# Last query and value stores on GpSimd's queue, the keys' rotation ahead of two reversed differences, and row differences one group sooner

## The chip, the core and the metric

The kernel runs on one core of one Trainium2 chip. The metric is device time in microseconds (us) of one execution. A core has a matrix engine (TensorE, "PE"), a vector engine ("DVE"), a scalar engine ("ACT"), GpSimd ("POOL") and SyncE ("SP"). Each of them works through its own list of instructions in order, and they wait for each other through semaphores. Transfers between the chip's memory (DRAM) and the on-chip memory (SBUF) are issued here by SP, ACT and POOL. Matrix products land in PSUM, in tiles (banks) of 128 partitions by 512 words.

## What is computed

The reference is one layer of a diffusion backbone, for 256 prompt tokens and 2048 latent tokens of width 1024. One projection gives queries, keys, values and Fourier channels. Four heads run differential attention; four groups of 128 channels go through a two-dimensional Fourier transform; both are joined, projected, and followed by a squared-ReLU MLP. Only these parts bear on the change:

```python
def project(h, w_in, q_g, k_g):
    p = h @ w_in
    q, k, v, f = jnp.split(p, [QK_WIDTH, 2 * QK_WIDTH, 2 * QK_WIDTH + ATTN_WIDTH], axis=-1)
    q = rms_norm(q.reshape(b, n, N_HEADS, 2, HEAD_DIM), q_g)
    k = rms_norm(k.reshape(b, n, N_HEADS, 2, HEAD_DIM), k_g)
...
def fourier_mix(f, w_four):
    spec = jnp.fft.fft2(f.astype(jnp.float32), axes=(1, 3), norm='ortho').real.astype(f.dtype)
    return jnp.einsum('bngc,gce->bnge', spec, w_four).reshape(b, n, FOUR_WIDTH)
```

Latent queries and keys are also rotated by their grid position ("axial rotary").

## The kernel before

The work is done in stages that follow each other on PE: setup and projection (to about 485 us), the Fourier transform (to about 559 us), attention, output projection and MLP. Each operand of a large product is split into a high and a low part (`hi` by a cast on ACT, `lo` by a subtraction on DVE), and `mm3` (lines 86 to 89) runs three products.

**Projection.** Tokens come in 18 tiles of 128. For each tile, `proj` (line 238) makes four 512-column groups: 0 queries, 1 keys, 2 values, 3 Fourier channels. `qk_norm` (266) and `qk_post` (272) normalise and rotate queries and keys on DVE: a small table product (292), a product (293), two half products (301) and an addition (303). `head_T` transposes them; `k_store` (317) and `q_store` (328) write the parts to DRAM, four and eight transfers of 128 KB, in pieces of 512 bytes. `v_post` (360) copies the values out of PSUM, splits them and issues three stores (357, 349).

**The last tile** (lines 560 to 649) has its order written out by hand. `manual_schedule()` fixes, for each engine, that the instructions of the region go in the order in which they are written. The region that follows (789 onward) has an order of its own; how the two are merged on an engine is left to the scheduler. In this stretch POOL loads the cosine and sine matrices of the 2048-point transform (`c_load`, `dft`, line 583), 512 KB each. SP loads the Fourier rows (`d_load`, 599) and stores keys and queries of the tile before the last (`k_store`, `q_store`, lines 619 and 620).

**Even and odd parts.** `e2048(t)` (624) takes a row tile and its mirror image `rv` and makes, on DVE, their difference (628) and sum (629), the sum in place of the mirror. ACT casts the difference (634), and DVE subtracts (635): the operands `E_h`, `E_l`. For t = 0, POOL copies one row into the sum (631). The tiles are taken in the order 3, 2, 0, 1 (`EROWS`).

**Fourier stage.** PE first multiplies the four even parts (line 827), for four channel groups, into four banks (`pabE`), and makes the group matrices (807, 808) in a fifth (`pabw`). The pool `ab` has five banks. The sums are split into `O_h`, `O_l` (831, by the helper at 578 and 579), first t = 0, the one with POOL's row. Then `e_evac` and `group_parts` empty banks, and the loop over groups (845) runs the odd products into a bank `pabo` (846). Meanwhile POOL loads ten smaller matrices (838), SP the prompt's rows (841) and eight tiles of row sums (`s_load`, 732). These eight share buffers with the cosine matrices, so each pair waits until PE has read the matrix before it.

**Preparation** for the shorter transforms is a list, `PREP` (774), of which `prep(n)` takes the next n entries: the prompt's two splits, four row differences (`diff`, 741), reversals by matrix product on PE (`reverse`, 755 and 756), sums (744), and even and odd parts made from the reversals (764, 765). The loop over groups calls `prep(2)` for g = 1 and 3; later loops call `prep(3)` for each prompt group and `prep(1)` for each later group (871). The stage ends where attention's first scores begin (line 969).

Of the kernel before, what the change touches and what calls it, by code (L numbers as in the profile page):

```python
# [19 lines left out]
P = 128  # L20
# [6 lines left out]
H = 4  # L27
# [10 lines left out]
def f32(ap):  # L38
    return ap.bitcast(F32)


def body(tc, a, out):
    nc = tc.nc
    ctx = ExitStack()
    with ctx:
# [6 lines left out]
        def scratch(name, shape):  # L52
            return dram.tile(shape, F32, tag=name, name=name)
# [3 lines left out]
        vs = scratch("vs", [NS, 512])  # L57
        NK = (PAST + NS, NP)
        kd = [scratch(f"kd{s}", [H, 2, P, NK[s]]) for s in range(2)]
        vd = [scratch(f"vd{s}", [H, P, NK[s] // P, 2, P]) for s in range(2)]  # L60
        qd = [scratch(f"qd{s}", [H, (NS, NP)[s] // 256, P, 2, 2, 256]) for s in range(2)]
# [24 lines left out]
        def mm3(ps, lh, ll, rh, rl, first, last):  # L86
            nc.tensor.matmul(ps, lh, rh, start=first, stop=False)  # L87
            nc.tensor.matmul(ps, lh, rl, start=False, stop=False)  # L88
            nc.tensor.matmul(ps, ll, rh, start=False, stop=last)  # L89
# [119 lines left out]
        with ExitStack() as c1:  # L209
# [6 lines left out]
            def t2(nm):  # L216
                return p1.tile([P, 512], F32, tag="t2", name=nm, bufs=6)

            def t2r(nm):
                return po.tile([P, 512], F32R, tag="t2r", name=nm, bufs=6)  # L220
# [17 lines left out]
            def proj(i, g):  # L238
                ps = pp.tile([P, 512], F32, tag="pj", name=f"pj{i}_{g}", bufs=4)
                hh, hl = HH[i]  # L240
                for k in range(KD):
                    mm3(ps, hh[:, k, :], hl[:, k, :], wh[g][k], wl[g][k], k == 0, k == KD - 1)
                PJ[i, g] = ps
# [81 lines left out]
                n = i if s else i - 2  # L325
                k_store(s, n if s else 4 + n, head_T(QK[i][1], f"kT{i}"))

            def q_store(i, hl):
                s = 1 if i < 2 else 0
                n = i if s else i - 2  # L330
                for m in range(2):
                    for x in range(2):
                        for d in range(2):
                            nc.sync.dma_start(qd[s][:, n // 2, d * 64:d * 64 + 64, x, m, n % 2 * P:n % 2 * P + P]
                                              .rearrange("h p k -> p h k"), hl[x][m * 64:m * 64 + 64])

            def q_T(i):
# [3 lines left out]
                k_T(i)  # L341
                q_T(i)

            def v_split(s, kt, src, nm):
                hi, lo = t2r(f"{nm}h"), t2r(f"{nm}l")
                nc.scalar.copy(hi, src)
                nc.vector.tensor_sub(lo, src, f32(hi))
                for x, t in enumerate((hi, lo)):
                    nc.sync.dma_start(vd[s][:, :, kt, x, :].rearrange("h p e -> p h e"), f32(t).rearrange("p (h e) -> p h e", h=H))

            def v_out(i):
                s = 1 if i < 2 else 0
                n = i if s else i - 2
                ps = PJ.pop((i, 2))
                o = t2(f"vo{i}")
                nc.scalar.copy(o, ps)
                nc.sync.dma_start(out[3][n * P:n * P + P] if s else vs[n * P:n * P + P], o)
                return o

            def v_post(i):  # L360
                s = 1 if i < 2 else 0
                n = i if s else i - 2
                o = v_out(i)
                v_split(s, n if s else 4 + n, o, f"v{i}")

            FH = {}

# [159 lines left out]
            wm, LAST = None, N1 - 1  # L527
# [32 lines left out]
            with tc.manual_schedule():  # L560
                rope_load(LAST)
                f_load(LAST)
                f_rev(LAST - 1)
                proj(LAST, 3)
                f_post(LAST)
                parts = [head_T(QK[LAST - 1][m], f"qkT{LAST - 1}_{m}") for m in (1, 0)]
                proj(LAST, 0)
                squares(LAST, 0, True)
                proj(LAST, 1)
                right.close()  # L570
                fa = right.enter_context(tc.tile_pool(name="f_a", bufs=2, side="right", reuse_waits="tile"))

                def ft32(pool, tag, nm, bufs):
                    return pool.tile([P, 512], F32, tag=tag, name=nm, bufs=bufs)

                def split(src, nm):
                    hi, lo = (ft32(fa, "src", f"{nm}{x}", 16).bitcast(F32R) for x in "hl")
                    nc.scalar.copy(hi, src)
                    V.tensor_sub(lo, src, f32(hi))
                    return hi, lo  # L580

                def dft(m, nm, t):
                    nc.gpsimd.dma_start(m, a[nm][t * P:t * P + P])
                    return m[:, 0, :], m[:, 1, :]


                ROWS, EROWS = (0, 1, 2, 3), (3, 2, 0, 1)
                src0 = [ft32(fa, "src", f"E{t}_{x}", 16) for t in EROWS for x in "hl"]
                etmp = [ft32(fa, "e", f"etmp{n}", 2) for n in range(2)]
                qko = [ft32(fa, "qo", f"qo{LAST}_{m}", 2) for m in range(2)]  # L590
                som = {t: fa.tile([P, 2, 512], F32R, tag="so", name=f"s2048{t}", bufs=4) for t in ROWS}
                DR = {t: (ft32(fa, "ds", f"ds{t}", 4), ft32(fa, "rv", f"rv{t}", 4)) for t in EROWS}
                com = {t: fa.tile([P, 2, 512], F32R, tag="co", name=f"c2048{t}", bufs=4) for t in EROWS}
                co, so = [None] * 4, [None] * 4
                c128, s128 = (fa.tile([P, P], F32, tag=x, name=x, bufs=1) for x in ("c128", "s128"))
                wf = fa.tile([P, 4, P], F32, tag="wf", name="wf", bufs=1)

                def d_load(t, x):
                    nc.sync.dma_start(DR[t][x], (fdif, frev)[x][t * P:t * P + P])

                def c_load(t):
                    co[t] = dft(com[t], "c2048", t)


                f_rev(LAST)
                for t in (3, 2):
                    d_load(t, 0)
                    d_load(t, 1)
                    c_load(t)
                nc.gpsimd.dma_start(c128, a["c128"])  # L610
                nc.gpsimd.dma_start(s128, a["s128"])
                nc.gpsimd.dma_start(wf, a["w_four"][0].rearrange("g p c -> p g c"))
                c_load(0)
                mid = p1.tile([P, 512], F32, tag="ff", name="mid", bufs=4)
                nc.sync.dma_start(mid[0:1, :], fdif[512:513])
                for x in range(2):
                    for t in (0, 1):
                        d_load(t, x)
                k_store(0, LAST + 1, parts[0])
                q_store(LAST - 1, parts[1])  # L620

                E, O = {}, {}

                def e2048(t):

                    d, r = DR[t]
                    e = t2(f"e2048_{t}")
                    V.tensor_sub(e, d, r)
                    V.tensor_add(r, d, r)
                    if t == 0:  # L630
                        nc.gpsimd.tensor_copy(r[0:1, :], mid[0:1, :])
                    n = 2 * EROWS.index(t)
                    hi, lo = (x.bitcast(F32R) for x in src0[n:n + 2])
                    nc.scalar.copy(hi, e)
                    V.tensor_sub(lo, e, f32(hi))
                    E[t] = hi, lo

                qk_post(LAST, (0,), qko)
                squares(LAST, 1, True)
                c_load(1)  # L640
                for t in ROWS:
                    so[t] = dft(som[t], "s2048", t)
                proj(LAST, 2)
                e2048(3)
                qk_norm(LAST, 1)
                for t in (2, 0, 1):
                    e2048(t)
                qk_post(LAST, (1,), qko)
                v_post(LAST)


        with ExitStack() as c2:
# [136 lines left out]
            with tc.manual_schedule():  # L789
# [55 lines left out]
                for g in range(4):  # L845
                    B = ab(g, 1, [O[t] for t in range(4)], so, 512, "o")
                    if g < 2:
                        e_evac(g + 2)
                    if pend:
                        put(2048)(*pend)  # L850
                    pend = g, A[g], B
                    if g in (0, 2):
                        parts[1 - g // 2] = head_T2(g // 2, ptq[g // 2])
                    if g % 2:
                        prep(2)
                last_put = put(2048)
                for n, (ea, ma, eb, mb), w, p in (
# [24 lines left out]
        with ExitStack() as c3_:  # L882
# [291 lines left out]
            for h in range(H):  # L1174
# [17 lines left out]
                for g in range(hd.ng):  # L1192
                    gr = Group(hd, g)
                    add(base - (4 if h or g > 1 else 3) * T + 0.6 * u if base else -3.03 * T, gr.qload)
                    for st in range(4):
                        j, m = divmod(st, 2)
# [210 lines left out]
        LAST = seq[-1]  # L1407
# [434 lines left out]
        with ExitStack() as c6:  # L1842
# [52 lines left out]
            for i in range(7):  # L1895
                for k in range(16):
                    n = i * 16 + k
# [7 lines left out]
            with tc.manual_schedule():  # L1905
                pend, NM, loaded, KS = None, 7 * 24, 4, []
                for i in range(7):
                    for b in range(3):
                        ps = [pp.tile([P, 512], F32, tag="ps", name=f"ps{i}_{b}_{j}", bufs=6) for j in range(3)]
                        for k in range(16):  # L1910
                            n, m = i * 16 + k, (i * 3 + b) * 8 + k // 2
# [24 lines left out]
                            if i == 0 and b == 1 and k in (2, 6, 10, 14):  # L1936
                                s, hf = divmod(k // 4, 2)
# [10 lines left out]
                for j in range(3):  # L1948
                    t = 6 + j
# [76 lines left out]
```

## Time and profile before

| | us |
|---|---|
| median of 3 runs | 2916.5 (2915.85 to 2916.76) |
| the profiled execution | 2920.95 |
| its span, first to last instruction | 2919.2 |
| PE busy | 2884.2 |
| DVE busy | 2018.9 |
| ACT busy | 1564.1 |
| POOL busy | 1044.6 |
| PE busy from 497.40 to 516.46 | 19.06 of 19.06 |
| PE busy from 516.46 to 558.94 | 37.90 of 42.48 |
| mean granted clock of PE | 0.998 |

All positions in us are counted from the start of the span. A row of the timeline has start, duration, engine, line, operation, the tile written and the tiles read, the count, and in brackets the idle time before it with what ended it. Rows are merged where equal instructions follow each other, so an interval can cover pauses. A row of the waits has who waited for whom, the total, the number and the longest. A row of the windows has the length, then busy time and count of PE, weight loads, DVE, ACT and POOL, then the granted clock of PE, the share of the transfer engines and GB/s. A name such as `SPq` is the queue of an engine: transfers that it issues, and its waits.

### The profile page before, as it was taken

What the parts mean: (1) busy time and instruction counts of PE and PEld (TensorE: products, weight loads), DVE (VectorE), ACT (ScalarE), POOL (GpSimd) and SP (SyncE); (2) the same over time, 40 slices, a digit from 0 to 9 for tenths busy, and PEclk for the clock granted to TensorE, in tenths of its full rate; (3) what the DMA queues carried; (4) which work ended last, traced back from release to release, by engine and by line L of the source; (5) the groups of instructions that cost most, each with busy time, mean ns of one, the idle gap of its engine ahead of it and who ended that gap; (6) DMA issues with size and microseconds to landing.
All of it is one profiled execution on the core that took longest, in us unless ns stands there. A gap on an engine that the chain in (4) does not pass through costs nothing.

```text
span 2919.2 us, 43814 instructions
## 1 busy us (share of the span) xinstructions
PE 2884.2 (99%) x15425; PEld 2505.5 (86%) x15425; DVE 2018.9 (69%) x3401; ACT 1564.1 (54%) x3524; POOL 1044.6 (36%) x849
## 2 busy tenths in 40 slices
PE   8999999999999999999999999999999999999999
PEld 4888888688888888888889999999998888888887
DVE  6666777888998988964468778778775344345554
ACT  4333323688998989964356566556554322232221
POOL 1111113199898999952213333333332000000000
PEclk9999999999999999999999999999999999999999
DMA  7777878611121201217776677676656354445663
GB/s 280 198 203 189 224 199 254 230 67 71 44 104 47 109 28 46 89 54 214 215 247 214 221 238 234 221 239 221 222 189 235 124 197 153 135 142 174 205 206 108
DMA packets 394415, 495.59 MB, mean 170 GB/s; under 512 B 26403, under 2 KB 307056, under 8 KB 391122
## 3 DMA queue, kind: packets, MB, share of 16 engines
q1 hardware_dynamic: 386560, 477.63, 51.3%
q0 software_dynamic: 2992, 7.28, 0.8%
q10 hardware_dynamic: 4642, 7.88, 0.8%
q8 instruction: 122, 2.00, 0.3%
q14 instruction: 99, 0.81, 0.1%
HBM read 315.20 MB, written 179.57 MB: 169 GB/s over the span
## 4 chain that ended last, share of the span: by engine, by line
PE 91%; DMA 3%; ACT 2%; DVE 2%; issue 1%; POOL 1%; SPq 0%; ACTq 0%; POOLq 0%; DVEq 0%
PE Ss L969 10%; PE ps L87 8%; PE ps L88 8%; PE ps L89 8%; PE pts L1024 5%; PE pj L89 4%; PE pj L87 4%; PE pj L88 4%; PE po L89 4%; PE po L87 4%; PE po L88 4%; PE pA L1634 2%; PE pA L1635 2%; PE pB L1634 2%; PE pB L1635 2%; PE pB L1636 2%
## 5 line engine op out<-in xcount | busy, mean ns | idle before, releaser
L974 DVE TENSOR_REDUCE mxs<-Ss 128x1 f32<-128x512 f32 x636 | 413.2, 685 | 65.5 <-PE Ss L969 52.7
L1309 DVE TENSOR_TENSOR sl<-sr,sh 128x768 fp32r<-128x768 f32 x168 | 161.7, 964 | 340.0 <-ACT sh L1308 339.5
L1009 POOL TENSOR_TENSOR P0s<-P0s,P1s 128x1024 f32<-128x1024 f32 (+2 forms) x128 | 377.2, 2947 | 10.7
L1308 ACT CAST sh<-sr 128x768 fp32r<-128x768 f32 x168 | 140.1, 835 | 424.9 <-PE ps L88 424.9
L1676 POOL TENSOR_TENSOR gs<-g,g 128x384 f32<-128x384 f32 x48 | 69.7, 1452 | 469.6 <-ACT g L1646 400.9
L993 ACT ACTIVATE P1s<-Ss,mxs 128x512 f32<-128x512 f32 x318 | 215.4, 695 | 35.6 <-DVE mxs L977 34.2
L87 PE MATMUL pj<-wh,hh 128*128 128x512 f32 x576 | 229.5, 399 | 0.7 <-ACT fo L381 0.7
L88 PE MATMUL ps<-tlT,sh 128*128 128x512 f32 x585 | 229.3, 392 | 0.0
L87 PE MATMUL ps<-thT,sh 128*128 128x512 f32 x585 | 229.2, 392 | 0.0
L88 PE MATMUL pj<-wl,hh 128*128 128x512 f32 x576 | 227.7, 395 | 0.5 <-DVE wl L503 0.5
L89 PE MATMUL ps<-thT,sl 128*128 128x512 f32 x585 | 227.7, 389 | 0.0
L89 PE MATMUL pj<-wh,hl 128*128 128x512 f32 x576 | 226.7, 394 | 0.0
L993 ACT ACTIVATE P0s<-Ss,mxs 128x512 f32<-128x512 f32 x318 | 214.3, 691 | 4.3 <-DVE mxs L977 3.7
L969 PE MATMUL Ss<-KS1s,Qs 128*128 128x512 f32 x636 | 196.3, 420 | 5.7 <-ACT P0s L993 3.1
L969 PE MATMUL Ss<-KS0s,Qs 128*128 128x512 f32 x636 | 196.5, 421 | 2.4 <-ACT P1s L993 2.4
L1024 PEld LDWEIGHTS pts<-ident,P0s 128*128 128x128 f32 x1280 | 158.2, 140 | 42.9 <-ACT ahs L1031 3.1
L1024 PE MATMUL pts<-ident,P0s 128*128 128x128 f32 x1280 | 191.2, 273 | 0.7 <-ACT P1s L993 0.7
L1645 ACT ACTIVATE g<-uz 128x384 f32<-128x384 f32 x144 | 75.8, 527 | 201.0 <-DVE uz L1668 175.0
L1008 POOL TENSOR_SCALAR P1s<-P1s,tots 128x1024 f32<-128x1024 f32 (+2 forms) x128 | 172.1, 1345 | 5.7
L1036 DVE TENSOR_TENSOR als<-pts,ahs 128x512 fp32r<-128x512 f32 x256 | 165.8, 681 | 6.9 <-ACT ahs L1031 6.6
L87 PE MATMUL ps<-ophT,sh 128*128 128x512 f32 x423 | 165.9, 392 | 1.1 <-DVE uz L1668 1.1
L89 PE MATMUL ps<-ophT,sl 128*128 128x512 f32 x423 | 165.7, 392 | 0.0
(640 smaller groups left out, 8202.4 us busy)
## 6 DMA issues: line engine op xcount, KB each, us to landing
sr<-sd SPq DMA_DIRECT2D x84, 768.0 KB, 4.5
a<-in_w SPq DMA_DIRECT2D x184, 256.0 KB, 4.3
sd<-gs SPq DMA_DIRECT2D x192, 192.0 KB, 2.0
sd<-g SPq DMA_DIRECT2D x144, 192.0 KB, 4.4
wm<-in_w_mod SPq DMA_DIRECT2D x32, 512.0 KB, 5.8
Qs<-qd SPq DMA_DIRECT2D x32, 512.0 KB, 3.4
b<-in_w SPq DMA_DIRECT2D x64, 256.0 KB, 5.1
b<-tsum SPq DMA_DIRECT2D x64, 256.0 KB, 4.7
```

The lines of the kernel that those rows point to most:

```text
L87: nc.tensor.matmul(ps, lh, rh, start=first, stop=False)
L88: nc.tensor.matmul(ps, lh, rl, start=False, stop=False)
L89: nc.tensor.matmul(ps, ll, rh, start=False, stop=last)
L969: nc.tensor.matmul(S[:, :w], self.Q[:, x, m, j * P:j * P + P], self.hd.KS[m][:, b * 512:b * 512 + w], start=(x == 0), stop=(x == 1))
L974: nc.vector.tensor_reduce(self.mx[j][:, m, b:b + 1], self.S[j, m, b], axis=AX.X, op=ALU.max)
L993: nc.scalar.activation(dst, S, AF.Exp, bias=self.mx[j][:, m, 6:7], accum_out=self.sm[j][:, m, b:b + 1])
L1008: nc.gpsimd.tensor_scalar(p, p, tot[:, 3:4], 0.0, op0=ALU.mult, op1=ALU.add)
L1009: nc.gpsimd.tensor_add(d, d, p)
L1024: nc.tensor.transpose(pt[:, c:c + P], self.p0[j][:, (kb + t) * P:(kb + t + 1) * P], ident)
L1036: nc.vector.tensor_sub(t, self.pt[kb], f32(self.A[kb][0]))
L1308: nc.scalar.copy(hi, src)
L1309: nc.vector.tensor_sub(lo, src, f32(hi))
```

## The change

Three edits:

1. `q_store`, `v_out`, `v_split` and `v_post` get a parameter for the issuing engine, SP by default. The query store of the tile before the last goes to POOL, and in the program's text it moves from behind `k_store` to behind the four sine loads. The three value stores of the last tile go to POOL too.
2. The keys' rotation, `qk_post(LAST, (1,), qko)`, moves from behind all four `e2048` to behind the second, ahead of those for t = 0 and t = 1.
3. `prep(2)` is called for g = 1, 2 and 3, not for 1 and 3. The list `PREP` and the later calls stay as they are.

```diff
-            def q_store(i, hl):
+            def q_store(i, hl, q=nc.sync):
...
-                            nc.sync.dma_start(qd[s][:, n // 2, d * 64:d * 64 + 64, x, m, n % 2 * P:n % 2 * P + P]
+                            q.dma_start(qd[s][:, n // 2, d * 64:d * 64 + 64, x, m, n % 2 * P:n % 2 * P + P]
...
-            def v_post(i):
+            def v_post(i, q=nc.sync):
...
-                o = v_out(i)
-                v_split(s, n if s else 4 + n, o, f"v{i}")
+                o = v_out(i, q)
+                v_split(s, n if s else 4 + n, o, f"v{i}", q)
...
                 k_store(0, LAST + 1, parts[0])
-                q_store(LAST - 1, parts[1])
...
                 c_load(1)
                 for t in ROWS:
                     so[t] = dft(som[t], "s2048", t)
+
+                q_store(LAST - 1, parts[1], nc.gpsimd)
                 proj(LAST, 2)
                 e2048(3)
                 qk_norm(LAST, 1)
-                for t in (2, 0, 1):
+                e2048(2)
+                qk_post(LAST, (1,), qko)
+                for t in (0, 1):
                     e2048(t)
-                qk_post(LAST, (1,), qko)
-                v_post(LAST)
+                v_post(LAST, nc.gpsimd)
...
-                    if g % 2:
+                    if g:
                         prep(2)
```

More of the change, by code (lines that the diff above doesn't have):

```diff
@@ L342, in qk_T, with v_split @@
                 q_T(i)
-            def v_split(s, kt, src, nm):
+            def v_split(s, kt, src, nm, q=nc.sync):
                 hi, lo = t2r(f"{nm}h"), t2r(f"{nm}l")
@@ L348, in v_split, with v_out @@
                 for x, t in enumerate((hi, lo)):
-                    nc.sync.dma_start(vd[s][:, :, kt, x, :].rearrange("h p e -> p h e"), f32(t).rearrange("p (h e) -> p h e", h=H))
-            def v_out(i):
+                    q.dma_start(vd[s][:, :, kt, x, :].rearrange("h p e -> p h e"), f32(t).rearrange("p (h e) -> p h e", h=H))
+            def v_out(i, q=nc.sync):
                 s = 1 if i < 2 else 0
@@ L356, in v_out @@
                 nc.scalar.copy(o, ps)
-                nc.sync.dma_start(out[3][n * P:n * P + P] if s else vs[n * P:n * P + P], o)
+                q.dma_start(out[3][n * P:n * P + P] if s else vs[n * P:n * P + P], o)
                 return o
-            def v_post(i):
+            def v_post(i, q=nc.sync):
                 s = 1 if i < 2 else 0
                 n = i if s else i - 2
-                o = v_out(i)
-                v_split(s, n if s else 4 + n, o, f"v{i}")
+                o = v_out(i, q)
+                v_split(s, n if s else 4 + n, o, f"v{i}", q)
             FH = {}
```

## The prediction

> **What bounds the kernel now.** I read the page first: the share of busy time, then the chain that ended last.
>
> ```profile
> PE 2884.2 (99%) x15425; PEld 2505.5 (86%) x15425; DVE 2018.9 (69%) x3401; ACT 1564.1 (54%) x3524; POOL 1044.6 (36%) x849
> PE 91%; DMA 3%; ACT 2%; DVE 2%; issue 1%; POOL 1%; SPq 0%; ACTq 0%; POOLq 0%; DVEq 0%
> ```
>
> The kernel is one long TensorE stream. An edit counts only where it opens or closes a gap in that stream, and all the edits lie in one stretch, from the last projection (about 470 us) to the first attention scores (558.94 us). So the next view is who keeps PE waiting there (window 497 to 560), then the chain of waits, merged, of that place, then PE's busy time and granted clock in some stretches.
>
> ```profile
> PE rev L755 <- DVE d L741: 2.0, 1, 2.0
> PE py L88 <- DVE able L697: 1.6, 1, 1.6
> PE py L88 <- DVE ablp L697: 0.3, 1, 0.3
> PE pabf L89 <- DVE o_0l L579: 0.2, 1, 0.2
> PE pabe L89 <- DVE e_1l L579: 0.2, 1, 0.2
> ```
>
> ```profile
> 500.61 10.20 DMA vd<-v17l
> 510.82 6.80 DMA ss<-fsum
> 517.64 0.70 DVE d L741
> 518.48 1.39 PE rev L755 x2
> ```
>
> ```profile
> 37.87:41.28 3.41, 2.72 (x10) 2.22 (x11) 3.24 (x7) 3.41 (x8) 0.00 (x0) 0.50 0.15 59
> 41.28:44.69 3.41, 3.41 (x9) 2.64 (x9) 3.41 (x7) 3.41 (x8) 0.00 (x0) 0.50 0.49 163
> 515.73:519.14 3.41, 1.40 (x6) 0.65 (x5) 1.50 (x3) 1.17 (x2) 0.00 (x0) 1.00 1.11 360
> 519.14:522.56 3.42, 3.42 (x10) 2.00 (x9) 1.66 (x4) 0.00 (x0) 0.00 (x0) 0.50 1.00 229
> 522.56:525.97 3.41, 3.41 (x20) 2.45 (x20) 2.46 (x5) 1.50 (x4) 0.00 (x0) 1.00 0.37 86
> ```
>
> The reader is to see one story. The reversal at L755 waits 2.0 us for a row difference, which waits for the last load of the sums, which was issued only when the last value store had landed. PE then pays twice: in the 3.41 us with only 1.40 us of work the clock is still 1.00, in the next 3.42 us it is 0.50. Half clock for 3.42 us costs 3.42/2 = 1.7 us. The first row is a warning: a stretch with 2.72 of 3.41 us busy did not bring the clock back, the fully busy one after it did.
>
> The Trainium skill, "TensorE: Matmul & The Clock Gate", section "Part 1: The HAM clock gate (the "warmup" mystery)", says that the clock halves after an idle window of about 3.4 us and returns after a busy one. By its idle rule the 2.0 us gap would be free of the 1.7 us, and the sum below would end 1.7 us higher; the rows above contradict it, so I charge the 1.7 us.
>
> **The change part by part.**
>
> *Stores off SP.* SP's rows, in order of time, show what the query stores hold up.
>
> ```profile
> 482.28 4.24 SPq L334 DMA_DIRECT2D qd<-qkT_0h  x2
> 496.71 1.72 SPq L334 DMA_DIRECT2D qd<-qkT_0l  x2
> 498.47 1.09 SPq L841 DMA_DIRECT2D etmp<-fp  x2
> 501.38 9.76 SPq L732 DMA_DIRECT2D ss<-fsum  x8
> ```
>
> The eight query stores hold SP from 482.28 to 498.43, and three value stores follow. Without them, the prompt loads (L841) can issue at about 482 and the sums (L732) as PE gives their buffers free, the last after 496.5 when PE has read the last cosine matrix, instead of 510.82. With the row's 6.8 us to landing the last sum is there near 505, before PE's wait that begins at 516.5. So the 2.0 us stall and the 1.7 us of half clock go: 3.7 us gained. What is late next is the DVE work below.
>
> *Differences one group sooner.* The same four subtractions are issued for groups 2 and 3, where DVE is idle in part (1.50 us busy of 3.41 in the row from 515.73), not for group 3 and the first prompt group.
>
> ```profile
> 517.64 1.29 DVE L741 TENSOR_TENSOR d<-ss,ss 128x512 f32<-128x512 f32 x2 [2.53 <-DMA ss<-fsum]
> 519.52 1.28 DVE L741 TENSOR_TENSOR d<-ss,ss 128x512 f32<-128x512 f32 x2
> ```
>
> ```profile
> 530.00:540.00 10.00, 7.79 (x58) 6.74 (x57) 9.84 (x20) 6.10 (x16) 0.00 (x0) 1.00 0.33 127
> ```
>
> This takes 1.28 us from DVE's queue behind the reversal and brings each later preparation forward. The later PE waits on DVE in this stage (1.6 + 0.3 and two of 0.2 us) sum to 2.3 us, so the bounds are 0 and 2.3 us. DVE is busy 9.84 of 10 us there, in its third column, and preparation brought forward stands in front of the evacuations that PE waits for, so waits move as well as go. I take 0.9 us, between the middle and the lower end.
>
> *Rotation of the keys ahead of two differences.* It costs what it cost before; only the last two even parts (L628 to L635) come later by its length, 492.85 - 490.39 = 2.5 us.
>
> ```profile
> 487.35 0.69 DVE L635 TENSOR_TENSOR E_l<-e,E_h 128x512 fp32r<-128x512 f32 x1
> 489.70 0.77 DVE L635 TENSOR_TENSOR E_l<-e,E_h 128x512 fp32r<-128x512 f32 x1
> 490.39 0.28 DVE L292 TENSOR_TENSOR tb<-rp,kg 128x128 f32<-128x128 f32 x1
> 492.10 0.82 DVE L303 TENSOR_TENSOR qo<-qo,qt 128x512 f32<-128x512 f32 x1
> 491.58 0.39 PE L89 MATMUL pabE<-c,E_l 128*128 128x512 f32 x1
> 494.30 0.39 PE L89 MATMUL pabE<-c,E_l 128*128 128x512 f32 x1
> ```
>
> The two low parts would end at 488.04 + 2.5 = 490.5 and 490.47 + 2.5 = 493.0; PE asks for them at 491.58 and 494.30. Cover of 1.1 and 1.3 us: cost nothing, up to 1 us if it fails.
>
> *Stores on POOL.* Here I see the price. The region fixes each engine's order as written. On POOL that is: the four sine loads, now eight query stores, then the one-row copy L631 (row 0 of the first odd part, inside the third `e2048`), then three value stores.
>
> ```profile
> 478.34 0.57 POOL L610 DMA_DIRECT2D c<-in_c  x1
> 479.40 0.82 POOL L612 DMA_DIRECT2D wf<-in_w_four  x1
> 486.59 1.06 POOL L583 DMA_DIRECT2D s<-in_s  x2 [1.48 <-DMA c<-in_c]
> 488.07 1.16 POOL L631 COPY rv<-mid 1x512 f32<-1x512 f32 x1
> 505.08 0.54 POOL L583 DMA_DIRECT2D c<-in_c  x1 [1.38 <-DMA c<-in_c]
> ```
>
> The issues are cheap: 0.57 us for 128 pieces of 512 bytes, 0.82 for 512, so about 0.65 for a query store's 256; 5.2 us for eight. But POOL also waits before issues. The tenth load of the first batch (486.59) waits for the landing of an earlier load; so does the ninth of the batch that starts at 499.40 (505.08). Both fit a limit of eight transfers under way for the queue, the ninth waiting for the first. The eight query stores come right behind the four sine loads, so the fifth to eighth wait for exactly these four. The landing times of the last two sine loads (L583, window 487.0 to 487.4) are:
>
> ```profile
> DMA to landing us min/median/max: 8.5/9.5/10.4
> ```
>
> The last is issued at 487.1 and lands 10.4 us later, at 497.5. So the eighth query store issues at 497.5, the copy runs from 498.15 to 499.3, and not from 488.07 to 489.23. Behind the copy stands this:
>
> ```profile
> 491.80 2.18 ACT L578 CAST O_h<-rv 128x512 fp32r<-128x512 f32 x4
> 494.73 0.59 ACT L696 CAST abhE<-pabE 128x512 fp32r<-128x512 f32 x1 [0.75 <-PE pabE L89]
> 494.06 2.68 DVE L579 TENSOR_TENSOR O_l<-rv,O_h 128x512 fp32r<-128x512 f32 x4
> 496.66 0.68 DVE L697 TENSOR_TENSOR ablE<-pabE,abhE 128x512 fp32r<-128x512 f32 x1
> 497.40 0.50 PE L87 MATMUL pabo<-s,O_h 128*128 128x512 f32 x1
> ```
>
> ACT's first odd cast needs the copied row, the other three and the first evacuation (abhE) queue behind it, and DVE's low parts behind them. PE's odd products start at 497.40 just after ablE ends, since all five accumulator banks are held until then. From the copy's end: 0.65 us to the first low part, 2.68 for four, 0.68 for ablE, so PE restarts at about 499.3 + 4.0 = 503.3: **5.9 us of stall**. No other PE work may pass. A gap this long, by the clock rows, brings half clock until one stretch of 3.41 us is wholly busy: 3.4 to 6.8 us, 1.7 to 3.4 us lost, less what falls into the gap; I take 2.6. POOL's later work (sign flips, value stores, the ten later matrix loads) moves with PE and is needed well after: nothing.
>
> The Trainium skill, "DMA: Bandwidth & Descriptors", section "Issuing engines are not separate DMA queues", says that issuing from another engine saves only the issuing time, since all transfers share the same engines. By that rule the stores move no faster from POOL; the sum already counts only SP's freed time, so it stays the same.
>
> **Sum**, against the profiled execution: 2920.95 us (span 2919.2 us). Loss 5.9 + 2.6 = 8.5; gain 2.0 + 1.7 + 0.9 = 4.6; net +3.9 us, 2924.9 us there. The median of the runs is 2916.5 us, 4.45 us below the profiled one, so 2920.4 us.
>
> **The rivals.**
>
> *No block (faster).* The copy is done by 493.4 us, that is 497.4 - 4.0, and nothing of PE's start moves. It decides whether the eighth store may issue before the sine loads land, for instance if the queue takes more than eight when they are stores. For it: the change's cover on DVE is sound and the 3.7 us are plain. Against it: two rows with waits of 1.48 and 1.38 us on loads. It gives 2916.5 - 4.6 = 2911.9 us, 2910.5 with all 2.3 us.
>
> *Long block (slower).* The sums and prompt loads now on SP compete with the sine loads, and the last lands later than 497.5. It decides from about 2 us later on: 5.9 + 2.0 + 3.4 - 3.7 (nothing from the earlier differences) = +7.6, 2924.1 us. For it: the transfer engines are full there (share 1.11 in the row from 515.73). Against it: ahead of those loads SP's key stores of 512-byte pieces still stand in the same queue, as before.
>
> *The change doesn't do what it says.* The scheduler may merge the following region's POOL and SP work differently, so that the sums do not come earlier or the copy comes 2 us sooner. Loss and gain then cancel to about nothing: 2916.5 us.
>
> **How the numbers follow.** Forecast (block, 0 to +5.8 us) 0.58; no block 0.20; long block 0.15; cancelled 0.07. The bound between same and different, 0.2%, is 5.8 us, about what a measurement of this kernel can tell from no change. Within it lie the forecast, the cancelled case and most of no block (0.58 + 0.07 + 0.16 = 0.81); faster keeps 0.04, slower 0.15. Range: without no block at most 0.80 is held, less the long block's tail, so it reaches from no block's own 2911.9, rounded out to 2911.8, to the long block's 2924.0. The likeliest case alone lies between 2916.5 and 2922.3.
>
> **What would show it.** Right: POOL waits of several us in all at L334 on the sine loads; copy L631 near 499 us; ACT's O_h waiting for POOL rv; PE's pabo waiting for DVE ablE, with clock 0.50 behind it; no wait of rev on d. The rotation: no PE wait at pabE. Wrong: L631 still before 493 us, or pabo starting near 497.4. The sum for the differences fails if able and ablp still make PE wait 2 us.

## The result, and the profile after

The changed kernel takes 2923.95 us, the median of 15 runs (2921.63 to 2925.35). The kernel before, in 15 runs beside it, takes 2918.76 us (2915.85 to 2921.69). The ratio is 1.0018, with a 95% interval of 1.001 to 1.0026: the change costs 5.2 us, and 2.9 to 7.6 us by the interval. The profiled executions are 2923.58 us after and 2920.95 us before.

The page of the kernel after, its busy times and the shares of the chain that ended last:

```profile
PE 2883.7 (99%) x15425; PEld 2505.8 (86%) x15425; DVE 2018.1 (69%) x3401; ACT 1562.5 (53%) x3524; POOL 1050.5 (36%) x860
PE 85%; issue 6%; POOL 3%; DVE 3%; ACT 3%; DMA 1%; SPq 0%; POOLq 0%; ACTq 0%; DVEq 0%
```

Only POOL has more work than before, 1050.5 us in 860 instructions against 1044.6 in 849: eleven more, as many as the stores that it now issues. The chain's shares differ from those before (PE 91%, DMA 3%, issue 1%, POOL 1%), but they do not show what happened: POOL has 0% in the experiment below with the stores alone, which loses time too, and 3% in the one with the copy first, which does not. Who keeps PE waiting from 497 to 562 us, all that the view lists:

```profile
PE pabo L87 <- DVE ablE L699: 5.6, 1, 5.6
PE py L88 <- DVE ablp L699: 0.8, 1, 0.8
PE py L87 <- ACT abhe L698: 0.6, 1, 0.6
PE py L88 <- DVE able L699: 0.4, 1, 0.4
```

The wait of `rev` for the row difference `d` (2.0 us before) is gone. In its place stands 5.6 us of the first odd product, `pabo`, for `ablE`. The timeline of POOL, ACT, DVE and PE shows where it comes from (rows left out are marked); the bracket is the engine's idle time and what ended it:

```profile
492.76 0.63 POOL L334 DMA_DIRECT2D qd<-qkT_0h  x1 [2.04 <-DMA s<-in_s]
494.17 0.63 POOL L334 DMA_DIRECT2D qd<-qkT_0h  x1 [0.78 <-DMA s<-in_s]
495.73 0.63 POOL L334 DMA_DIRECT2D qd<-qkT_0l  x1 [0.93 <-DMA s<-in_s]
497.32 0.63 POOL L334 DMA_DIRECT2D qd<-qkT_0l  x1 [0.95 <-DMA s<-in_s]
498.38 0.60 POOL L630 COPY rv<-mid 1x512 f32<-1x512 f32 x1
...
499.01 2.18 ACT L578 CAST O_h<-rv 128x512 fp32r<-128x512 f32 x4 [5.87 <-POOL rv L630]
499.66 2.77 DVE L579 TENSOR_TENSOR O_l<-rv,O_h 128x512 fp32r<-128x512 f32 x4 [5.68 <-ACT O_h L578]
502.35 0.68 DVE L699 TENSOR_TENSOR ablE<-pabE,abhE 128x512 fp32r<-128x512 f32 x1
503.08 0.79 PE L87 MATMUL pabo<-s,O_h 128*128 128x512 f32 x1 [5.57 <-DVE ablE L699]
```

Read it from the bottom. PE waits 5.57 us for DVE, DVE waited 5.68 us for ACT, ACT 5.87 us for one row that POOL copies, and POOL waited four times for the landing of a sine load before it could issue a query store. It is one delay, handed down through four engines.

PE's busy time and granted clock in this stretch (columns as before: length, PE, weight loads, DVE, ACT, POOL, clock, transfer share, GB/s):

```profile
495.02:498.43 3.41, 2.49 (x16) 2.02 (x14) 0.00 (x0) 0.00 (x0) 1.75 (x6) 1.00 1.05 374
498.43:501.85 3.42, 0.00 (x0) 0.00 (x0) 2.19 (x4) 2.84 (x6) 3.42 (x7) 1.00 1.04 399
501.85:505.26 3.41, 2.18 (x5) 1.79 (x6) 2.37 (x4) 0.79 (x2) 3.29 (x9) 0.50 1.05 405
505.26:508.68 3.42, 3.42 (x10) 2.54 (x10) 0.00 (x0) 0.08 (x1) 3.14 (x6) 0.50 1.15 374
508.68:512.10 3.42, 3.42 (x18) 2.88 (x17) 1.89 (x3) 1.68 (x4) 1.07 (x2) 1.00 1.29 379
```

After the empty stretch the clock is 0.50 for two stretches. PE works in them from 503.08 to 508.68, so it loses 5.60/2 = 2.8 us. The counts agree: 10 products in a full stretch at 0.50, 18 at 1.00.

What the change was to gain is in two more rows of the timeline of after:

```profile
487.58 13.14 SPq L734 DMA_DIRECT2D ss<-fsum  x8
519.27 1.28 DVE L743 TENSOR_TENSOR d<-ss,ss 128x512 f32<-128x512 f32 x2
```

The loads of the sums are issued from 487.58 us, not from 501.38, and the first differences start with no idle time ahead of them.

### The profile page after: what moved, and what is told of

Its sections match the earlier page's. It is cut to its first block, busy times and chain, and to the rows that moved or that the text cites. A ratio compares the mean times of both kernels' runs of the same rounds, so it can differ in the third digit from the quotient of the medians.

```text
span 2921.8 us, 43817 instructions
## 1 busy us (share of the span) xinstructions
PE 2883.7 (99%) x15425; PEld 2505.8 (86%) x15425; DVE 2018.1 (69%) x3401; ACT 1562.5 (53%) x3524; POOL 1050.5 (36%) x860
## 4 chain that ended last, share of the span: by engine, by line
PE 85%; issue 6%; POOL 3%; DVE 3%; ACT 3%; DMA 1%; SPq 0%; POOLq 0%; ACTq 0%; DVEq 0%
PE Ss L971 10%; PE ps L87 8%; PE ps L88 8%; PE ps L89 8%; PE pts L1026 5%; PE pj L89 4%; PE pj L87 4%; PE pj L88 4%; PE po L87 4%; PE po L89 4%; PE po L88 4%; PE po L1052 2%; PE pA L1636 1%; PE pA L1637 1%; PE pA L1638 1%
```

## The experiments

**Theory.** The slowdown is the block: the one-row copy stands behind eight query stores on POOL, and the last four wait for the sine loads. Without it the change would gain. **Rivals.** The stores cost time wherever they stand on POOL's queue (because transfers crowd each other there), or the reordering on DVE costs it, and the stall merely shows there. The first seven experiments were timed in 11 runs each. Beside the copy ahead of the stores, the copy on DVE, the stores alone and the order alone stand 33 runs of the kernel before (median 2918.59 us), beside the other three 27 (2919.9 us). A ratio is to the kernel before beside it, with its 95% interval; it can differ from the quotient of the two medians by up to 0.0003. Diffs are against the changed kernel where nothing else is said.

**The copy ahead of the stores.** Everything of the change stays; only the query stores are written behind the last `e2048`, so that the copy goes first.

```diff
-                q_store(LAST - 1, parts[1], nc.gpsimd)
                 proj(LAST, 2)
...
                     e2048(t)
+                q_store(LAST - 1, parts[1], nc.gpsimd)
                 v_post(LAST, nc.gpsimd)
```

> The change with one move: the eight query stores are written behind the four even parts, so that POOL's one-row copy stands ahead of them; they stay on POOL. Theory (block: the copy waits in POOL's order behind stores that wait for the sine loads): the copy runs before 492 us, the odd products start near 497.4 us with no wait, and the 5.6 us stall and the 2.8 us of half clock go while the gain from SP stays: about 4 us below before, ratio 0.9986, some 8 us below the change. Rival 1 (late rotation: the keys' rotation delays the even and odd parts): the wait at the odd products stays near 5 us, ratio as the change, 1.0018. Rival 2 (POOL's queue: the stores cost on POOL wherever they stand, by late matrix loads behind them): PE waits later, at the prompt products, for some us; ratio 1.000 to 1.002.

It takes 2915.32 us, ratio 0.9988 (0.998 to 0.9997). The timeline of POOL, then PE's waits from 497 to 562 us (one of attention's left out):

```profile
490.64 1.04 POOL L630 COPY rv<-mid 1x512 f32<-1x512 f32 x1 [0.60 <-DVE rv L628]
...
498.65 0.63 POOL L334 DMA_DIRECT2D qd<-qkT_0l  x1 [0.92 <-DMA s<-in_s]
```

```profile
PE py L88 <- DVE ablp L699: 0.9, 1, 0.9
PE py L88 <- DVE able L699: 0.7, 2, 0.4
PE py L87 <- ACT abhe L698: 0.6, 1, 0.6
```

The stores still wait for the sine loads, and the last is issued later than in the changed kernel, at 498.65 us. Nothing that PE waits for stands behind them: the wait of `pabo` is gone. Each against the kernel before that was timed beside it, the changed kernel stands at +5.2 us (2.9 to 7.6) and this one at -3.3 (-5.8 to -0.9), so by the medians the place of one copy is worth 8.5 us. The transfers themselves cost nothing that can be seen.

**The copy on DVE.** The change as it is, but the one row is copied by DVE, where it waits for no store.

```diff
-                        nc.gpsimd.tensor_copy(r[0:1, :], mid[0:1, :])
+                        V.tensor_copy(r[0:1, :], mid[0:1, :])
```

> The change with the one-row copy on DVE in place of POOL; POOL's stores stay behind the sine loads. Theory (block): POOL's waits of some 5 us on the sine loads stay as they are, but nothing that PE needs stands behind them; DVE has 0.4 us more, hidden; no wait at the odd products, about 4 us below before, ratio 0.9986. Rival 1 (late rotation): the wait stays, ratio 1.0018. Rival 2 (POOL's queue): PE waits later for matrices loaded behind the stores, ratio 1.000 to 1.002.

It takes 2915.34 us, ratio 0.9991 (0.9982 to 1.0). POOL's waits between 483 and 512 us:

```profile
POOL qd L334 <- DMA s<-in_s: 3.3, 4, 0.9
POOL qd L334 <- DMA c<-in_c: 2.9, 2, 2.4
```

POOL waits as long as in the changed kernel (6.2 us in all, against 4.7 + 1.2), in the same place, and PE does not wait for `ablE` at all. So it is not the stores' waiting that costs, but what stands behind it in POOL's list. This settles the theory from the other side.

**Four stores ahead of the copy, four behind.** If only the fifth to eighth store wait for the sine loads, four may stay in front.

```diff
-            def q_store(i, hl, q=nc.sync):
+            def q_store(i, hl, q=nc.sync, ms=range(2)):
...
-                for m in range(2):
+                for m in ms:
...
-                q_store(LAST - 1, parts[1], nc.gpsimd)
+                q_store(LAST - 1, parts[1], nc.gpsimd, (0,))
...
                     e2048(t)
+                q_store(LAST - 1, parts[1], nc.gpsimd, (1,))
```

> The change with the eight query stores cut in two: four stay behind the sine loads, four are written behind the even parts and so behind POOL's one-row copy. Theory (a limit of eight transfers under way: store n waits for the landing of the transfer eight places before it, and the first four wait only for the two 64 KB matrices, the group weights and a cosine matrix, all landed by about 490 us): the copy runs at about 490.7 to 492, and PE waits less than 0.5 us at the odd products; time as with the copy first, ratio 0.9988. Rival (stores on this queue wait for all loads ahead of them): the fourth store does not issue before 497 us, and the stall of some 5 us stays, ratio 1.0015 or more.

It takes 2915.24 us, ratio 0.9983 (0.9974 to 0.9992), the lowest ratio of the study. POOL's timeline:

```profile
491.96 0.63 POOL L334 DMA_DIRECT2D qd<-qkT_0l  x1 [0.86 <-DMA c<-in_c]
493.02 0.60 POOL L630 COPY rv<-mid 1x512 f32<-1x512 f32 x1
494.45 0.64 POOL L334 DMA_DIRECT2D qd<-qkT_0h  x1 [0.83 <-DMA s<-in_s]
```

The fourth store still waits for a cosine load and the fifth for a sine load, which is what a limit of eight transfers under way gives. Whether the limit belongs to the chip or to the program that builds the kernel is not shown. The copy ends at 493.62 us and PE waits 0.2 us for `ablE`; the prediction's "done by 493.4 us" was the right bound. This version and the one with the copy first beat both kernels.

**The stores alone.** The rotation and the differences are put back.

```diff
-                e2048(2)
-                qk_post(LAST, (1,), qko)
-                for t in (0, 1):
+                for t in (2, 0, 1):
                     e2048(t)
+                qk_post(LAST, (1,), qko)
...
-                    if g:
+                    if g % 2:
                         prep(2)
```

> The kernel before with the stores of the change alone: query and value stores on POOL behind the sine loads; rotation and differences as before. Theory (block): PE waits 5 to 6 us at the odd products behind ablE, half clock follows, the wait for the row difference is gone; about +4 to +5 us, ratio 1.0015 to 1.002. Rival 1 (late rotation): no wait at the odd products, about -4 us, ratio 0.9987. Rival 2 (POOL's queue): as the theory in time, but PE's wait stands at a later place.

It takes 2922.85 us, ratio 1.0017 (1.0009 to 1.0026). PE's two longest waits:

```profile
PE pabo L87 <- DVE ablE L698: 5.3, 1, 5.3
PE py L88 <- DVE able L698: 1.5, 1, 1.5
```

The stores alone bring the loss and the block. The wait of 1.5 us for `able`, which is 0.4 us in the full change, shows what the earlier differences are for.

**The order alone.** The stores are put back on SP; rotation and differences stay as changed.

```diff
                 k_store(0, LAST + 1, parts[0])
+                q_store(LAST - 1, parts[1])
...
-                q_store(LAST - 1, parts[1], nc.gpsimd)
...
-                v_post(LAST, nc.gpsimd)
+                v_post(LAST)
```

> The kernel before with the rotation and the differences of the change, all stores on SP as before. Theory (block): no wait at the odd products; the last sum still lands at 517.6 us, and two differences now stand on DVE ahead of the evacuation of the fourth odd product, so the 2.0 us wait moves to that product's use and grows by 1 to 2 us, with half clock behind it: +0 to +2 us, ratio 1.0000 to 1.0007. Rival 1 (late rotation): a wait of about 5 us at the odd products, ratio 1.0015 or more.

It takes 2920.12 us, ratio 1.0004 (0.9995 to 1.0013). The longest wait of PE and then of DVE, both from 497 us on:

```profile
PE pz L88 <- DVE ablo L698: 3.2, 1, 3.2
```

```profile
DVE d L742 <- DMA ss<-fsum: 4.0, 1, 4.0
```

The differences are one group sooner, but the sums still land late. DVE takes its list in order, so it sits 4.0 us before the difference, and the evacuation `ablo` behind it is late for PE by 3.2 us. Without the earlier loads the edit gains nothing that the runs can tell.

**Differences back, copy first.** As the first experiment, with `prep(2)` at g = 1 and 3 again (diff against the first experiment).

```diff
-                    if g:
+                    if g % 2:
                         prep(2)
```

> The copy-first kernel with the differences back at groups 1 and 3. Theory (the gain comes from the sums' early landing; the differences' place is worth at most the rest of the DVE waits): no wait for a row difference of 2 us, DVE waits of 2.0 to 2.5 us in the preparation; 0 to 1 us above the copy-first kernel, ratio to before 0.9988 to 0.9992. Rival (the differences' place is what closes the gap): the 2 us wait at the reversal is back, ratio near 1.0000.

It takes 2916.92 us, ratio 0.9993 (0.9984 to 1.0002), 1.7 us above the four-and-four version beside it. PE's longest wait:

```profile
PE py L88 <- DVE able L699: 1.5, 1, 1.5
```

**Rotation back, copy first.** As the first experiment, with the rotation last again (diff against the first experiment).

```diff
-                e2048(2)
-                qk_post(LAST, (1,), qko)
-                for t in (0, 1):
+                for t in (2, 0, 1):
                     e2048(t)
+                qk_post(LAST, (1,), qko)
```

> The copy-first kernel with the keys' rotation back behind all four even parts. Theory (the rotation's place is worth nothing either way): same waits at the same places, within 0.5 us of the copy-first kernel, ratio to before 0.9988. Rival (the rotation ahead shortens the way to the first transposes or delays the even parts): a difference of 1 us or more, with a wait that appears or goes at the even products.

It takes 2916.34 us (2914.86 to 2920.1), ratio 0.9991 (0.9982 to 0.9999). In this stage PE waits 0.8, 0.6 and 0.4 us for `ablp`, `abhe` and `able`, as in the changed kernel. The rotation's place is worth nothing that the runs can tell.

**The kernel before, three more profiles.** The gain side of the sum came from one profiled execution. Are its 2.0 us wait and the half clock behind it there in every execution? No edit.

> The kernel before, unchanged, for a second profile. Theory (the half clock follows a grid of 3.41 us stretches that lies differently in each execution): the waits of PE stand at the same places with the same lengths, among them three of 2.0 to 2.2 us, but not each of them is followed by half clock; the time follows their number, 1.7 us for each stretch. Rival (a wait of 2 us always costs half clock): the same spells of 6.8, 3.4 and 3.4 us as in the first profile.

It takes 2920.71 us. PE's three longest waits from 497 to 562 us, and one of DVE's from 470 to 500 us:

```profile
PE pabo L87 <- DVE ablE L697: 2.0, 1, 2.0
PE py L88 <- DVE able L697: 1.5, 1, 1.5
PE rev L755 <- DVE d L741: 1.1, 1, 1.1
```

```profile
DVE e L628 <- DMA rv<-frev: 2.8, 1, 2.8
```

The same program waits elsewhere: a mirror load of Fourier rows landed 2.8 us late for DVE and brought a short block of its own, and `rev` waits 1.1 us, with no half clock behind it. My expectation of equal places and lengths failed.

> The kernel before, a third profiled execution. Open: in one profile of it the reversal waits 2.0 us for a row difference and half clock follows (1.7 us); in the other the wait is 1.1 us with no half clock behind it, but the odd products start 2.0 us late, because the third mirror load landed 2.8 us later. Theory A (the wait for the difference is there in every execution, with 1 to 2 us, and the half clock behind it only in some, by where the gap falls in the clock's 3.4 us stretches; the late mirror load is an accident of one execution): rev waits 1.0 to 2.1 us for d, ablE makes PE wait less than 0.3 us, half clock behind rev or not. Theory B (the first profile is the rule): rev waits 2.0 us and half clock follows for 3.4 us. Theory C (the second profile is the rule): pabo waits 2 us for ablE again.

It takes 2920.81 us. PE's waits from 497 to 566 us (others left out):

```profile
PE pz L87 <- DVE ys L683: 1.6, 1, 1.6
...
PE rev L755 <- DVE d L741: 0.8, 1, 0.8
PE pabo L87 <- DVE ablE L697: 0.8, 1, 0.8
```

And one of DVE's, from 470 to 500 us:

```profile
DVE e L628 <- DMA rv<-frev: 0.9, 1, 0.9
```

> The kernel before, a fourth profiled execution; the same three theories as for the third. Theory A: rev waits 1.0 to 2.1 us for d, no wait of pabo above 0.3 us, half clock behind rev in some of the executions. Theory B: 2.0 us and half clock again. Theory C: pabo waits 2 us for ablE.

It takes 2918.34 us. PE's two longest waits:

```profile
PE py L88 <- DVE able L697: 1.5, 1, 1.5
PE rev L755 <- DVE d L741: 1.0, 1, 1.0
```

In four profiles `rev` waits 2.0, 1.1, 0.8 and 1.0 us, and only the first has half clock behind it. In the third `pabo` waits 0.8 us, which none of my three theories allowed (A had at most 0.3, and at least 1.0 for `rev`). The wait of 1.6 us for `ys` there comes from the sums too: DVE stood 4.22 us before that `ys`, until a load of the sums had landed (1.98 us in the first profile, at no cost to PE). The fourth fits theory A, and is the nearest to the median of 2918.76 us.

**The changed kernel, once more.** No edit.

> The changed kernel, a second profiled execution. Theory: the block is in every execution, since a gap of over 5 us holds a whole stretch of 3.4 us or nearly: pabo waits 5.2 to 6.0 us for ablE, half clock for 3.4 to 6.8 us behind it, no wait of rev for d. Rival: the length of the block goes with the landing of the last sine load and moves by over 1 us between executions, and the half clock is missing in some.

It takes 2926.19 us. PE's longest wait, POOL's timeline, and one of PE's stretches:

```profile
PE pabo L87 <- DVE ablE L699: 7.0, 1, 7.0
```

```profile
496.51 0.63 POOL L334 DMA_DIRECT2D qd<-qkT_0h  x1 [2.44 <-DMA s<-in_s]
...
499.29 0.63 POOL L334 DMA_DIRECT2D qd<-qkT_0l  x1 [0.85 <-DMA s<-in_s]
```

```profile
503.94:507.35 3.41, 2.25 (x5) 1.83 (x6) 2.30 (x4) 0.67 (x2) 3.29 (x8) 0.50 1.05 404
```

The block is there again with half clock behind it, but the rival was right about its length: the last store is issued at 499.29 and not at 497.32 us, and the stall is 7.0 us, not 5.6. The length goes with the landing of the loads; that the half clock can be missing, the rival's second part, did not show.

## Why the prediction came out as it did

**The block: right.** Forecast were the eighth store at 497.5 us, the copy's end at 499.3, PE's restart at 503.3 and a stall of 5.9 us. Measured are 497.32, 498.98, 503.08 and 5.57. Two small errors cancel there: three fills of the next region went ahead of the copy (from 497.94 to 498.38 us), and the copy took 0.60 us, not 1.16. The half clock was put at 2.6 us and is 2.8. Loss forecast 8.5 us; by the medians of the changed kernel and of the copy ahead of the stores it is 8.5, but with their intervals so close an agreement is luck; by the first column of the table below it is 7.3 to 9.8 us, against the 18.84 us before. The chain of reasons (limit of eight, stores behind loads, one-row copy behind stores, ACT, DVE, PE) is shown by the two experiments that take the copy from behind the stores and by the four-and-four one. Its length is not fixed: the stall is 5.3 to 7.0 us in three profiles with the block.

The other terms can be read from PE's stream, cut at the same four of its instructions in every profile: the last product of the group matrices (`pabw`), the last `pz` product ahead of the first reversal, the first `pabp` product with a sine matrix behind that reversal, and attention's first scores. In the first profile of the kernel before these start at 497.24, 516.08, 522.62 and 558.94 us, in the changed kernel at 497.12, 524.32, 526.95 and 562.19. The lengths in us, by profile:

| kernel | odd products | first reversal | rest of the stage |
|---|---|---|---|
| before, four profiles | 18.84, 21.62, 21.81, 18.85 | 6.54, 4.02, 3.71, 3.89 | 36.32, 36.53, 36.33, 36.22 |
| changed, two profiles | 27.20, 28.60 | 2.63, 2.63 | 35.24, 35.69 |
| stores alone | 26.14 | 2.63 | 36.28 |
| copy first | 19.08 | 2.63 | 35.77 |
| copy on DVE | 18.99 | 2.63 | 35.29 |
| four and four | 19.25 | 2.63 | 35.62 |
| rotation back, copy first | 19.19 | 2.62 | 35.63 |
| differences back, copy first | 19.22 | 2.62 | 36.27 |
| order alone | 22.84 | 5.12 | 34.29 |

**The gain: about the right size, but not made up as I said.** I took 2.0 + 1.7 us for certain, since one profile of before showed them. The second column has 6.54 - 2.63 = 3.9 us for that profile, but 1.1 to 1.4 us for the three others. Two of these lose 2.8 to 3.0 us among the odd products in its stead, behind late mirror loads and a late load of the sums, and no kernel with the copy out of the way shows that (18.99 to 19.25 us). So the total was right in part by luck. By the medians the change with the copy first gains 3.3 us (0.9 to 5.8 by the interval), the four-and-four version 4.7, against 4.6 forecast.

**The differences: 0.9 us forecast, about 0.8 measured.** The last column has 36.22 to 36.53 us in the six profiles with the old place and 35.24 to 35.77 in the six with the new one, the order alone left out, where the waits stand elsewhere. The two groups do not overlap, and their means differ by 0.8 us. That the edit makes PE wait where the loads are late (3.2 us in the order alone) I had not seen.

**The rotation: nothing, as forecast.** No PE wait at `pabE` in the changed kernel.

**The net and the absolute time: too low.** Forecast +3.9 us and 2920.4, measured +5.2 and 2923.95. Of the 3.55 us between, 2.26 are the base: "The median of the runs is 2916.5 us" rested on three runs, and fifteen give 2918.76. The other 1.3 us are the net. They lie in the gain and not in the loss, as far as medians tell, but the intervals are too wide to prove it.

**The step that failed** is the last one, "the bound between same and different, 0.2%, is 5.8 us, about what a measurement of this kernel can tell from no change". I put 0.81 within it. The change costs 0.18%, inside that bound, yet the runs tell it from no change, since their interval is 0.1% to 0.26%. A forecast of +3.9 us, 0.13%, was a forecast of slower and should have been called so. In the sum, the term that was mis-sized is the 2.0 + 1.7 us at the reversal: 1.1 to 1.4 us against three of the four profiles of the kernel before. Two further parts fell: the long block was weighed as a rival of its own, where executions of the changed kernel move between the two, and "no block" had 0.20 with two quoted waits against it.

In the pair of profiles the table gives the account of this stage: +8.36 us among the odd products (5.57 of stall and 2.8 of half clock), -3.91 at the reversal, -1.08 behind it, and -0.12 since the first cut lies that much sooner. This is the +3.25 us by which attention's first scores come later.

## What to carry to other kernels

Before moving transfers to another engine, list what stands behind them in that engine's order: a DMA issue that must wait for a free place holds every later instruction, and a one-row copy can be the one that counts. Ask whose landing each issue waits for; the fix here was to let the small instruction go first, at no cost. Profile the kernel before more than once, since a wait of 2 us in one execution may be 1 us in the next.

## What was not expected of the hardware

**When the clock halves.** Within an execution the stretches in which the clock changes lie on a fixed grid: in the kernel before, from 37.87 to 515.73 us are 140 stretches of 3.413 us. Two pauses of 2.0 us at about the same place ended differently. The first fence has two stretches of the second profile of before, with 1.81 and 0.19 us idle; the next has two of the fourth, with all 2.00 us in one:

```profile
588.49:591.90 3.41, 1.60 (x9) 0.96 (x7) 2.90 (x6) 2.38 (x8) 3.32 (x3) 1.00 0.22 47
591.90:595.31 3.41, 3.22 (x18) 2.60 (x19) 2.59 (x5) 3.41 (x12) 3.24 (x3) 1.00 0.29 112
```

```profile
585.32:588.73 3.41, 1.41 (x7) 0.83 (x6) 3.10 (x6) 2.38 (x7) 3.23 (x4) 1.00 0.34 112
588.73:592.14 3.41, 3.41 (x12) 2.66 (x11) 1.52 (x3) 2.79 (x9) 3.33 (x3) 0.50 0.12 47
```

With 1.60 us of work in the stretch the clock stayed at 1.00, with 1.41 us the next stretch was at 0.50. The stretch from 515.73 us in the first profile of before, with half clock behind it, had 1.40 us. In all 13 profiles of this case the pause near this place (about 580 to 597 us) goes the same way: in eight of them a stretch held 1.41 or 1.42 us of work and half clock followed, in five none held less than 1.60 us and the clock stayed. So the same gap costs 1.7 us or nothing, by where the grid cuts it, and executions of one kernel differ by that. The Trainium skill, "TensorE: Matmul & The Clock Gate", section "Part 1: The HAM clock gate (the "warmup" mystery)", says that the window is 3413 ns long and free-running, which these rows bear out; its idle window of about 3.4 us they do not: a stretch with 1.4 us of work was enough.

**How much a landing moves.** In four profiles of the kernel before a mirror load was 2.8 us late for DVE in one, 0.9 us in another and not late in two. In two of the changed kernel the last of the eight stores was issued at 497.32 or 499.29 us. The cause of this spread was not looked into.
